# Two-layer hybrid trunk, fp32 as split words: the feed-forward layers in blocks of two weight strips with the activations stationary, in three parts of the inner width, and SBUF opened stage by stage

## The chip, the cores and the metric

The kernel runs on one core of a Trainium2 chip. The metric is the device time of one execution in microseconds (us). The core has five engines that work at the same time and wait for each other by semaphores: TensorE (PE, the matrix array; its weight loads are listed apart as PEld), VectorE (DVE), ScalarE (ACT), GpSimd (POOL) and SyncE (SP, which here only issues DMAs).

## The reference

A decoder trunk of two layers over 256 tokens of width 2048, all float32. Layer 0 mixes by an mLSTM group and a Mamba-2 group from one input projection, layer 1 by causal attention. Each layer ends in a feed-forward layer of inner width 5632, and this is what the change is about:

```python
def rms_norm(x, g):
    y = x * lax.rsqrt(jnp.mean(x * x, axis=-1, keepdims=True) + NORM_EPS)
    return y * g

def swiglu(x, w_gate, w_up, w_down):
    return (jax.nn.silu(x @ w_gate) * (x @ w_up)) @ w_down
...
    x = x + mixer(rms_norm(x, norm_mix[layer]), ...)
    x = x + swiglu(rms_norm(x, norm_ffn[layer]), *ffn_params[layer])
return rms_norm(x, final_norm)
```

## The kernel before

Every matrix product is done with both operands split into a high and a low word, each in a 32-bit format that PE takes in one pass: `wh` is a cast of the weight on ACT (L204), `wl` the remainder on DVE (L205), and activations are split likewise. A product is high times high, high times low and low times high, summed in PSUM. So PE spends three passes on each, and every weight of the 484 MB of matrices is read once, cast once and subtracted once. A chunk is 256 rows by 512 columns of weights (`chunk`, one DMA of 512 KB on SP's queue, four raw buffers, three of `wh` and of `wl`). The normed gain goes into the activations when they are transposed; the factor per token comes after the product.

There are two ways to multiply a chunk. `lin_w` holds the weights stationary: for each 128 weight columns and each 128 rows one matmul of `wh` over 512 columns (high and low words of the 256 tokens side by side, L219) and one of `wl` over 256 columns (L221); the result has channels on partitions, in four banks. `lin_a` holds the activations stationary: for each half of the tokens and each 128 rows three matmuls over the strip's 512 columns (L249 to L251); the result has tokens on partitions, in two banks.

In a feed-forward layer (`ffn`) 11 strips of gate and of up go through `lin_w`, so that the product of the two comes out with channels on partitions, ready to be the stationary operand of the down projection (`project_add` in layer 0, the last loop in layer 1), which is `lin_a` over all 5632 rows for each of four output strips. `project_add` adds the residual (L621), squares the sum on ACT for the next norm (`sq`, L257), transposes the strip on PE (`p_tr`, L169) and, at the end, `row_norm` turns the 256 factors into a row: POOL's power (L110), a diagonal on DVE (`dg`, L188), a matmul with ones (`p_rb`, L189) and a copy.

What is issued in which order is set by the program order together with a scheduler: the weights' casts carry a priority that lets them go ahead of other work of their engine by up to 800 instructions, if their buffers are free, and `later`/`tick` put small jobs (transposes, attention steps) between chunks. SBUF is one pool of 17 blocks of 8 KB per partition (`act`) beside the weight buffers (`stg`), PSUM a ring of six accumulator banks and one of two auxiliary banks. The Mamba gate weights `wg` are set to zero on POOL (L336), loaded by three DMAs of POOL (L338) and split at L341 (`wgh` on ACT, `wgl` on DVE).

## Time and profile before

| | |
|---|---|
| time, median of 3 runs | 2657.42 us (2655.51 to 2658.36) |
| the profiled execution | 2657.61 us |
| its span in the trace | 2655.8 us |
| PE busy | 2634.2 us, 99% of the span |
| DVE, ACT, POOL busy | 61%, 50%, 2% |
| DMA | 187 GB/s on average |
| matmul records on PE | 13765 |
| first matmul of gate/up a, down a, qkv, gate/up b, down b | 787.22, 1287.12, 1529.39, 1916.51, 2407.06 us |

All times of rows are us from the start of the span of that one profiled execution. A matmul's own duration is longer than its share of PE, since matmuls overlap in the array: what one costs is the distance from its start to the next one's start. The chain that ended last shows such shares directly.

### The profile page before, as it was taken

Reading aid. Unit: us, or ns where it says so; the run is one execution under the profiler, and the core shown is the slowest. Engines: PE = TensorE matmul, PEld = TensorE weight load, DVE = VectorE, ACT = ScalarE, POOL = GpSimd, SP = SyncE. Lnnn points to the kernel's source line nnn. Section 1 sums busy time; section 2 is a strip of 40 time slices with the busy share of each in tenths; the row PEclk is TensorE's granted clock in tenths of the full one; section 3 lists DMA queues with packets and bytes.
Section 4 is the critical chain, followed back from the end, with each engine's and each line's share of the span. In section 5 each row is a group of like instructions: output and inputs, shape, how many; then the busy total and the mean of one; then the engine's idle time right before and its main releaser. Section 6 shows DMA issues by size and latency. Waiting matters only on the chain.

```text
span 2655.8 us, 35559 instructions
## 1 busy us (share of the span) xinstructions
PE 2634.2 (99%) x13765; PEld 2246.7 (85%) x13765; DVE 1621.2 (61%) x2128; ACT 1335.1 (50%) x1906; POOL 45.8 (2%) x97
## 2 busy tenths in 40 slices
PE   8999999999999999999999999999999999999998
PEld 7888888888888888888888888888888888888887
DVE  6675687755456666666544466666566666665454
ACT  5465565665444444444444455556444444444443
POOL 1000010000000000000000000000000000000000
PEclk9999999999999999999999999999999999999999
DMA  7565656566555555555555565554556666665554
GB/s 231 168 191 182 184 182 204 167 187 219 189 190 182 185 188 185 188 184 189 190 191 190 190 182 169 177 171 163 185 183 190 190 190 190 190 190 206 193 195 160
DMA packets 254345, 496.86 MB, mean 187 GB/s; under 512 B 15656, under 2 KB 16048, under 8 KB 253792
## 3 DMA queue, kind: packets, MB, share of 16 engines
q1 hardware_dynamic: 250816, 484.57, 57.2%
q0 software_dynamic: 2896, 8.51, 1.1%
q8 instruction: 108, 1.77, 0.3%
q10 hardware_dynamic: 464, 1.52, 0.2%
q14 instruction: 61, 0.50, 0.1%
HBM read 492.39 MB, written 2.14 MB: 186 GB/s over the span
## 4 chain that ended last, share of the span: by engine, by line
PE 97%; DVE 1%; DMA 1%; issue 0%; ACT 0%; POOL 0%; SPq 0%; ACTq 0%; POOLq 0%; DVEq 0%
PE acc_w L219 35%; PE acc_w L221 18%; PE acc_a L249 13%; PE acc_a L251 13%; PE acc_a L250 13%; PE p_tr L169 1%; PE p_y L574 1%; DVE wl L205 1%; PE p_num L451 0%; DMA raw<-in_l_w_in 0%; PE p_qk L689 0%; PE p_o L719 0%; DMA xin<-in_x 0%; ACT wh L204 0%; PE p_pt L711 0%
## 5 line engine op out<-in xcount | busy, mean ns | idle before, releaser
L205 DVE TENSOR_TENSOR wl<-raw,wh 128x1024 fp32r<-128x1024 f32 (+1 forms) x913 | 1116.7, 1223 | 928.0 <-ACT wh L204 923.0
L204 ACT CAST wh<-raw 128x1024 fp32r<-128x1024 f32 (+1 forms) x913 | 958.9, 1050 | 1150.2 <-PE acc_w L219 551.0
L219 PE MATMUL acc_w<-x,wh 128*128 128x512 f32 x3328 | 1170.8, 397 | 0.0
L221 PE MATMUL acc_w<-x,wl 128*128 128x256 f32 x3328 | 929.1, 279 | 0.0
L219 PEld LDWEIGHTS acc_w<-x,wh 128*128 128x128 f32 x3328 | 624.8, 188 | 149.8
L221 PEld LDWEIGHTS acc_w<-x,wl 128*128 128x128 f32 x3328 | 626.9, 188 | 0.5
L219 PE MATMUL acc_w<-xa,wh 128*128 128x512 f32 x768 | 275.8, 403 | 1.1 <-DVE xa L118 1.1
L221 PE MATMUL acc_w<-xa,wl 128*128 128x256 f32 x768 | 215.9, 283 | 0.0
L219 PEld LDWEIGHTS acc_w<-xa,wh 128*128 128x128 f32 x768 | 145.0, 189 | 34.0 <-ACT wh L204 1.5
L249 PE MATMUL acc_a<-wh,xa 128*128 128x512 f32 x384 | 151.5, 395 | 0.0
L250 PE MATMUL acc_a<-wl,xa 128*128 128x512 f32 x384 | 150.8, 393 | 0.0
L251 PE MATMUL acc_a<-wh,xa 128*128 128x512 f32 x384 | 150.7, 393 | 0.0
L221 PEld LDWEIGHTS acc_w<-xa,wl 128*128 128x128 f32 x768 | 145.6, 190 | 1.0
L249 PE MATMUL acc_a<-wh,ha 128*128 128x512 f32 x352 | 137.5, 391 | 0.0
L251 PE MATMUL acc_a<-wh,ha 128*128 128x512 f32 x352 | 137.0, 389 | 0.0
L250 PE MATMUL acc_a<-wl,ha 128*128 128x512 f32 x352 | 137.0, 389 | 0.0
L249 PE MATMUL acc_a<-wh,hb 128*128 128x512 f32 x352 | 136.9, 389 | 0.0
L251 PE MATMUL acc_a<-wh,hb 128*128 128x512 f32 x352 | 136.9, 389 | 0.0
L250 PE MATMUL acc_a<-wl,hb 128*128 128x512 f32 x352 | 136.9, 389 | 0.0
L249 PE MATMUL acc_a<-wh,mx 128*128 128x512 f32 x256 | 100.4, 392 | 0.0
L251 PE MATMUL acc_a<-wh,mx 128*128 128x512 f32 x256 | 99.7, 390 | 0.0
L250 PE MATMUL acc_a<-wl,mx 128*128 128x512 f32 x256 | 99.6, 389 | 0.0
(240 smaller groups left out, 2514.0 us busy)
## 6 DMA issues: line engine op xcount, KB each, us to landing
raw<-in_l_w_in SPq DMA_DIRECT2D x191, 512.0 KB, 3.5
raw<-in_l_ffn_gate SPq DMA_DIRECT2D x176, 512.0 KB, 3.5
raw<-in_l_ffn_up SPq DMA_DIRECT2D x176, 512.0 KB, 3.5
raw<-in_l_ffn_down SPq DMA_DIRECT2D x176, 512.0 KB, 4.4
raw<-in_l_w_qkv SPq DMA_DIRECT2D x96, 512.0 KB, 3.6
raw<-in_l_w_out SPq DMA_DIRECT2D x64, 512.0 KB, 4.6
raw<-in_l_w_o SPq DMA_DIRECT2D x32, 512.0 KB, 3.5
rows<-scr POOLq DMA_DIRECT2D x10, 512.0 KB, 6.0
```

The costliest lines, as they stand in the source:

```text
L169: nc.tensor.transpose(pt[:, j * T + t * P:j * T + (t + 1) * P], src[t][:, c:c + P], ident)
L204: nc.scalar.copy(wh[:, ks, :], raw[:, ks, :])
L205: nc.vector.tensor_sub(wl[:, ks, :], raw[:, ks, :], wh[:, ks, :].bitcast(F32))
L219: nc.tensor.matmul(banks[f], wh[:, kk, fs], kt.both(k), start=k == 0, stop=False, skip_group_check=True)
L221: nc.tensor.matmul(banks[f][:, :T], wl[:, kk, fs], kt.parts(k)[0], start=False, stop=k == nk - 1, skip_group_check=True)
L249: nc.tensor.matmul(banks[t], xh[:, ts], wh[:, kk, :], start=k == 0, stop=False)
L250: nc.tensor.matmul(banks[t], xh[:, ts], wl[:, kk, :], start=False, stop=False)
L251: nc.tensor.matmul(banks[t], xl[:, ts], wh[:, kk, :], start=False, stop=k == nk - 1)
L574: nc.tensor.matmul(py[:, o0:o0 + SHD], e[:, lo:lo + P], y[st][:, hs], start=st == 0, stop=st == t, skip_group_check=True)
```

## The change

Gate and up strips of the same index are done together by `block`: per chunk of 256 rows, one tile of 1 MB is filled by two DMAs of 512 KB (256 rows of the gate strip, 256 of the up strip) and cast in two halves; then for each half of the tokens and each of the two strips, two times three matmuls over 512 columns with the activations stationary. The four products have a fixed bank each (F0 to F3: tokens 0 gate, tokens 0 up, tokens 1 gate, tokens 1 up). The hidden values now have tokens on partitions; so two tanh on ACT (L815) and four operations on DVE (L816, L817) read the banks, and 8 transposes on PE per strip, in two groups of four that are put behind the first chunks of the next block, bring the result back to channels on partitions.

The inner width is done in parts of 4, 4 and 3 strips: hidden values of a part, then the down projection over that part for all four output strips (two blocks of two strips), its result added to the residual after each part. `project_add` remains for `w_out` and `w_o`; the factors per token are used as a column there, so `row_norm` goes after these two. The pools become six long-lived blocks (`res`) and stages m, f, a, g, whose weight buffers and blocks lie over each other's addresses. The final gain is loaded in four pieces on ACT's queue, and the last block takes its last two chunks together. The file also has code for summed weight chunks; with every entry of `PLAN_X` and `PLAN_H` at "P" none of it is run, and it is left out below.

```diff
-    stg = ctx.enter_context(tc.tile_pool(name="stg", bufs=3))
-    act = ctx.enter_context(tc.tile_pool(name="act", bufs=17))
+    res = ctx.enter_context(tc.tile_pool(name="res", bufs=6))
...
-    psa = ctx.enter_context(tc.tile_pool(name="psa", bufs=6, space=PSUM))
-    psx = ctx.enter_context(tc.tile_pool(name="psx", bufs=2, space=PSUM))
+    psm = ctx.enter_context(tc.tile_pool(name="psm", bufs=1, space=PSUM))
...
+    def open_stage(name, act_bufs):
+
+        close_stage()
+        stage["guards"] = [tc.tile_pool(name="stg" + name, bufs=3, reuse_waits="tile"),
+                           tc.tile_pool(name="act" + name, bufs=act_bufs, reuse_waits="tile")]
+        stage["stg"], stage["act"] = [guard.__enter__() for guard in stage["guards"]]
+
     def blk(shape, name, dt=F32):
-        return act.tile(shape, dt, tag="blk", name=name)
+        return stage["act"].tile(shape, dt, tag="blk", name=name)
+
+    def long(shape, name, dt=F32):
+        return res.tile(shape, dt, tag="res", name=name)
 
...
+    def bank(i, name):
+        return psm.tile([P, 512], F32, tag=f"b{i}", name=name)
+
+    def next_bank(kind, name):
+        turn[kind] += 1
+        return bank(ring[kind][(turn[kind] - 1) % len(ring[kind])], name)
+
     def acc_bank(name):
-        return psa.tile([P, 512], F32, tag="acc", name=name)
+        return next_bank("acc", name)
 
     def aux_bank(name):
-        return psx.tile([P, 512], F32, tag="aux", name=name)
+        return next_bank("aux", name)
+
+    open_stage("m", 10)
 
...
+    def weights(src, row, summed):
+
+        pool = stage["stg"]
+        raw = pool.tile([P, 4, STRIP], F32, tag="raw", name="raw", bufs=4)
+        for i, (w, col) in enumerate(src):
+            nc.sync.dma_start(raw[:, 2 * i:2 * i + 2, :],
+                              w[row:row + 2 * P, col:col + STRIP].rearrange("(a p) f -> p a f", p=P))
+
+        def parts(of, cuts):
+            h = pool.tile([P, 4, STRIP], F32R, tag="wh", name="wh")
+            l = pool.tile([P, 4, STRIP], F32R, tag="wl", name="wl")
+            for c in cuts:
+                nc.scalar.copy(h[:, c, :], of[:, c, :])
+            for c in cuts:
+                nc.vector.tensor_sub(l[:, c, :], of[:, c, :], h[:, c, :].bitcast(F32))
+            return h, l
+
+        with tc.high_priority(offset=800):
+            if not summed:
+                return parts(raw, (slice(0, 2), slice(2, 4)))
...
+    def block(src, kt, row, nk, plan, after_sums=None, lead=1):
+        n = nk // 2
+        plan = plan[:n]
...
+        def add(dst, a, b, start, stop):
+            (ah, al), (bh, bl) = a, b
+            nc.tensor.matmul(dst, ah, bh, start=start, stop=False)
+            nc.tensor.matmul(dst, ah, bl, start=False, stop=False)
+            nc.tensor.matmul(dst, al, bh, start=False, stop=stop)
+
...
+                group.append((j, weights(src, row + 2 * j * P, False)))
+                if len(group) < lead and j < n - 1 and n - j <= lead:
+                    continue
+                for i in range(4):
+                    t, s = divmod(i, 2)
+                    first = F[i] is None
+                    if first:
+                        F[i] = bank(i, "acc_f")
+                    for jj, (wh, wl) in group:
+                        for kk in range(2):
+                            xh, xl = kt.parts(2 * jj + kk)
+                            ts = slice(t * P, (t + 1) * P)
+                            add(F[i], (xh[:, ts], xl[:, ts]), (wh[:, 2 * s + kk, :], wl[:, 2 * s + kk, :]),
+                                start=first and jj == group[0][0] and kk == 0, stop=jj == n - 1 and kk == 1)
+                group = []
+            tick()
+        return F, pre
...
+    def col_norm(name, ss4):
+
+        ss = sml.tile([P, NT], F32, tag="ss", name="ss" + name)
+        nc.vector.tensor_reduce(ss, ss4, axis=AX.X, op=OP.add)
+        r = cst.tile([P, NT], F32, name="r" + name)
+        rsqrt_mean(r, ss, D)
+        return r
+
...
+        return nx, col_norm(name, ss)
+
+    def ffn(xt, r, wg_, wu_, wd, name, finish, begin=None):
+
+        rh = cst.tile([P, NT], F32, tag="rh", name="rh" + name)
+        rr = cst.tile([P, NT], F32, tag="rr", name="rr" + name)
+        nc.vector.tensor_scalar(rh, r, 0.5, None, op0=OP.mult)
+        nc.vector.tensor_mul(rr, rh, r)
+
+        def hidden(hT, i, s, plan):
+            F, pre = block(((wg_, s * STRIP), (wu_, s * STRIP)), xt, 0, KD, plan)
+            hs = []
+            for t in range(NT):
+                g, u = F[2 * t], F[2 * t + 1]
...
+                h = t2([P, STRIP], "h")
+                nc.scalar.activation(h, g, AF.Tanh, scale=rh[:, t:t + 1])
+                nc.vector.scalar_tensor_tensor(h, h, 1.0, g, op0=OP.add, op1=OP.mult)
+                nc.vector.scalar_tensor_tensor(h, u, rr[:, t:t + 1], h, op0=OP.mult, op1=OP.mult)
+                hs.append(h)
+            transpose_later(hT, i, hs, None, 1)
+
+        def down(hT, first, n, last):
+            for q in range(2):
+                c0 = 2 * q * STRIP
+                dst = [xr_[t][:, c0 + n_ * STRIP:c0 + (n_ + 1) * STRIP] for t in range(NT) for n_ in range(2)]
+
+                def add_all(what):
+                    for d, x in zip(dst, what):
+                        nc.vector.tensor_add(d, d, x)
+
+                if last and begin is not None:
+                    begin(2 * q)
+                    begin(2 * q + 1)
+                F, _ = block(((wd, c0), (wd, c0 + STRIP)), hT, first * STRIP, 4 * n, PLAN_H, add_all,
+                             lead=2 if last and q and name == "b" else 1)
+                add_all(F)
+                if last:
+                    for s in (2 * q, 2 * q + 1):
+                        finish(s)
+
+        ring["aux"] = (6, 7)
+        first = 0
+        for n in (4, 4, 3):
+            hT = KT(f"h{name}{first}", 4 * n)
...
+            for i in range(n):
+                hidden(hT, i, first + i, PLAN_X if first + i else "P" * len(PLAN_X))
+                ring["aux"] = (4, 5, 6, 7)
+            down(hT, first, n, first + n == DFF // STRIP)
+            first += n
+        ring["aux"] = (6, 7)
+        turn["acc"] = 4
+
+    xt1, r1 = project_add(a["l0_w_out"], mixed, 32, "1", G_FFN0)
+    open_stage("f", 4)
...
+    ffn(xt1, r1, a["l0_ffn_gate"], a["l0_ffn_up"], a["l0_ffn_down"], "a", finish_ffn0)
+    r2, rb2_ = row_norm("2", ss2)
...
+    open_stage("a", 10)
...
+    xt3, r3 = project_add(a["l1_w_o"], oT, KD, "3", G_FFN1)
+    open_stage("g", 4)
+
+
+    gain = {}
+
+    def begin_ffn1(s):
+        gain[s] = stage["stg"].tile([P, STRIP], F32, tag="gf", name="gf", bufs=2)
+        fsrc = a["final_norm"]
+        nc.scalar.dma_start(gain[s], bass.AP(tensor=fsrc.tensor, offset=fsrc.offset + s * STRIP, ap=[[0, P], [1, STRIP]]))
+
     ssf = [cst.tile([P, 4], F32, name=f"ssf{t}") for t in range(NT)]
-    for s in range(4):
-        banks = lin_a(a["l1_ffn_down"], s * STRIP, h1, DFF // P, lead=3 if s == 3 else 1)
+
+    def finish_ffn1(s):
         cs = slice(s * STRIP, (s + 1) * STRIP)
         for t in range(NT):
-            nc.vector.tensor_add(xr_[t][:, cs], xr_[t][:, cs], banks[t])
             sumsq(ssf[t][:, s:s + 1], xr_[t][:, cs])
-            nc.vector.tensor_mul(xr_[t][:, cs], xr_[t][:, cs], gf[:, cs])
+            nc.vector.tensor_mul(xr_[t][:, cs], xr_[t][:, cs], gain[s])
+
+    ffn(xt3, r3, a["l1_ffn_gate"], a["l1_ffn_up"], a["l1_ffn_down"], "b", finish_ffn1, begin_ffn1)
```

On ACT, at the border from `w_out` to the first feed-forward layer (`raw` is the weights as loaded, `xres` the residual, `x13` the transposed last strip). Before:

```order
L204 CAST wh_6924<-raw_6923 128x1024
L204 CAST wh_6969<-raw_6968 128x1024
L204 CAST wh_7001<-raw_7000 128x1024
L204 CAST wh_7032<-raw_7031 128x1024
L257 ACTIVATE sq_6943,ss1_5686<-xres0_5682 128x512
L257 ACTIVATE sq_6945,ss1_5686<-xres1_5683 128x512
L204 CAST wh_7054<-raw_7053 128x1024
```

After:

```order
L266 CAST wh_6928<-raw_6927 128x1024
L418 ACTIVATE sq_6947,ss1_5690<-xres0_5686 128x512
L418 ACTIVATE sq_6949,ss1_5690<-xres1_5687 128x512
L147 ACTIVATE x13_7007<-p_tr_7008,pv_94 128x256
L147 ACTIVATE x13_7007<-p_tr_7050,pv_94 128x256
L147 ACTIVATE x13_7007<-p_tr_7008,pv_94 128x256
L147 ACTIVATE x13_7007<-p_tr_7050,pv_94 128x256
L329 CAST wh_6973<-raw_6970 128x1024 x2
L329 CAST wh_7020<-raw_7017 128x1024 x2
```

The first casts of the feed-forward weights stood ahead of the last squares, and now stand behind them and behind the four splits of the last strip.

On PE, at the same border. Before:

```order
L251 MATMUL acc_a_6633<-wh_6924,mx7_5779 128x512
L219 MATMUL acc_w_6964<-x10_6022,wh_6969 128x512
L221 MATMUL acc_w_6964<-x10_6022,wl_6970 128x256
L219 MATMUL acc_w_6964<-x10_6022,wh_6969 128x512
L221 MATMUL acc_w_6964<-x10_6022,wl_6970 128x256
```

After:

```order
L313 MATMUL acc_a_6637<-wh_6928,mx7_5783 128x512
L202 MATMUL p_tr_7008<-ident_86,xres0_5686 128x128
L202 MATMUL p_tr_7050<-ident_86,xres0_5686 128x128
L202 MATMUL p_tr_7008<-ident_86,xres1_5687 128x128
L202 MATMUL p_tr_7008<-ident_86,xres0_5686 128x128
L202 MATMUL p_tr_7008<-ident_86,xres1_5687 128x128
L202 MATMUL p_tr_7050<-ident_86,xres1_5687 128x128
L202 MATMUL p_tr_7050<-ident_86,xres0_5686 128x128
L202 MATMUL p_tr_7050<-ident_86,xres1_5687 128x128
L357 MATMUL acc_f_6979<-wh_6973,x10_6026 128x512
L357 MATMUL acc_f_6993<-wh_6973,x10_6026 128x512
L358 MATMUL acc_f_6979<-wl_6974,x10_6026 128x512
```

The first feed-forward matmuls stood right behind the last of `w_out`; now the eight transposes of the last strip stand between, and the three words of one product are no longer next to each other at first.

On DVE, some 25 us after the start, in the first input projection (`xa2` is the third strip of the transposed input, `dg` the diagonals, `wgl` the low word of the Mamba gate weights). Before:

```order
L118 SCALAR_TENSOR_TENSOR xa2_222<-p_tr_232,pv_90,xa2_222 128x256
L118 SCALAR_TENSOR_TENSOR xa2_222<-p_tr_223,pv_90,xa2_222 128x256
L188 TENSOR_SCALAR dg_389<-ident_82,r0_384 128x128
L188 TENSOR_SCALAR dg_392<-ident_82,r0_384 128x128
L205 TENSOR_TENSOR wl_283<-raw_281,wh_282 128x1024
L118 SCALAR_TENSOR_TENSOR xa2_222<-p_tr_232,pv_90,xa2_222 128x256
```

After:

```order
L148 SCALAR_TENSOR_TENSOR xa2_226<-p_tr_236,pv_94,xa2_226 128x256
L250 TENSOR_SCALAR dg_393<-ident_86,r0_388 128x128
L250 TENSOR_SCALAR dg_396<-ident_86,r0_388 128x128
L447 TENSOR_SCALAR rh0_401<-r0_388 128x2
L145 TENSOR_TENSOR wgl_1048<-wg_1042,wgh_1047 128x1536
L267 TENSOR_TENSOR wl_287<-raw_285,wh_286 128x1024
L267 TENSOR_TENSOR wl_328<-raw_326,wh_327 128x1024
L148 SCALAR_TENSOR_TENSOR xa2_226<-p_tr_227,pv_94,xa2_226 128x256
```

The subtraction for `wgl`, which came some 60 instructions later, moved in front, and one split of `xa2` moved behind it and two weight subtractions.

## Rows read from the trace of the kernel before

**Rows 1.** The page: busy time and share of the span of each engine, then the chain that ended last by engine, then one group of DMA issues (count, size, median us from issue to landing).

```profile
PE 2634.2 (99%) x13765; PEld 2246.7 (85%) x13765; DVE 1621.2 (61%) x2128; ACT 1335.1 (50%) x1906; POOL 45.8 (2%) x97
...
PE 97%; DVE 1%; DMA 1%; issue 0%; ACT 0%; POOL 0%; SPq 0%; ACTq 0%; POOLq 0%; DVEq 0%
...
raw<-in_l_ffn_gate SPq DMA_DIRECT2D x176, 512.0 KB, 3.5
```

**Rows 2.** PE alone in four stretches, gate/up a, down a, gate/up b, down b: from and to, length, PE busy (matmuls), granted clock, DMA share, GB/s.

```profile
800.00:1280.00 480.00, 480.00 (x2719) 1.00 0.59 186
1300.00:1525.00 225.00, 225.00 (x1005) 1.00 0.57 191
1930.00:2400.00 470.00, 470.00 (x2713) 1.00 0.61 190
2410.00:2640.00 230.00, 230.00 (x1016) 1.00 0.57 192
```

**Rows 3.** Groups of instructions in 800 to 1280 us (gate/up a): line, engine, operation, tiles, shapes, count | busy us, mean ns | idle before.

```profile
L219 PE MATMUL acc_w<-x,wh 128*128 128x512 f32 x1359 | 480.2, 399 | 0.0
L221 PE MATMUL acc_w<-x,wl 128*128 128x256 f32 x1360 | 382.0, 281 | 0.0
L643 DVE TENSOR_TENSOR sg<-sg,rb 128x512 f32<-128x512 f32 x22 | 15.1, 687 | 0.4
L641 ACT ACTIVATE thf<-sg 128x512 f32<-128x512 f32 x22 | 13.9, 630 | 0.6
```

**Rows 4.** The chain that ended last, in down a and at the end of `w_out`: start, length, work.

```profile
787.15 0.24 PE acc_a L251
...
791.41 0.68 PE p_rb L189 x4
...
1349.86 0.44 PE p_tr L169 x4
1353.07 0.44 PE p_tr L169 x4
```

**Rows 5.** The border from `w_out` to gate/up a in order of time: start, length, engine, line, operation [idle before and what ended it].

```profile
784.70 1.05 ACT L204 CAST wh<-raw 128x1024 fp32r<-128x1024 f32 x1 [1.67 <-PE acc_a L251]
...
786.93 1.28 DVE L621 TENSOR_TENSOR xres<-xres,acc_a 128x512 f32<-128x512 f32 x2
...
788.38 0.62 ACT L257 ACTIVATE sq<-xres 128x512 f32<-128x512 f32 x1
788.50 1.22 DVE L205 TENSOR_TENSOR wl<-raw,wh 128x1024 fp32r<-128x1024 f32 x1 [0.30 <-ACT wh L204]
...
791.41 0.68 PE L189 MATMUL p_rb<-dg,ones 128*128 128x128 f32 x4 [0.86 <-DVE dg L188]
...
792.86 0.46 ACT L117 ACTIVATE x<-p_tr,pv 128x256 fp32r<-128x256 f32 x1
...
793.35 0.48 DVE L118 SCALAR_TENSOR_TENSOR x<-p_tr,pv,x 128x256 fp32r<-128x256 f32 x1 [0.75 <-ACT x L117]
```

**Rows 6.** The border from down a to qkv, in the same form.

```profile
1529.10 1.28 DVE L621 TENSOR_TENSOR xres<-xres,acc_a 128x512 f32<-128x512 f32 x2
...
1533.51 0.68 PE L189 MATMUL p_rb<-dg,ones 128*128 128x128 f32 x4 [0.79 <-DVE dg L188]
```

**Rows 7.** The start in order of time, in the same form.

```profile
24.01 0.83 ACT L117 ACTIVATE xa<-p_tr,pv 128x256 fp32r<-128x256 f32 x2
...
25.41 2.09 DVE L188 TENSOR_SCALAR dg<-ident,r 128x128 f32<-128x128 f32 x2
...
25.95 1.40 POOL L336 MEMSET wg<- 128x1536 f32 x1
...
27.42 1.21 DVE L205 TENSOR_TENSOR wl<-raw,wh 128x1024 fp32r<-128x1024 f32 x1
...
27.50 0.40 PE L219 MATMUL acc_w<-xa,wh 128*128 128x512 f32 x1
```

**Rows 8.** The instructions that split the Mamba gate weights, by tile: line, engine, operation and count, duration min/median/max in ns, first and last start, shapes.

```profile
L114 ACT CAST wgh<-wg x1: 1478/1478/1478, 89.9 to 89.9; 128x1536 fp32r<-128x1536 f32 x1
L115 DVE TENSOR_TENSOR wgl<-wg,wgh x1: 1759/1759/1759, 91.4 to 91.4; 128x1536 fp32r<-128x1536 f32 x1
```

**Rows 9.** The chain at the start, in the form of rows 4.

```profile
10.82 2.08 PE acc_w L219 x4
...
13.53 1.28 PE acc_w L219 x3
...
16.98 0.93 PE acc_w L219 x4
```

**Rows 10.** The end of the kernel in order of time, in the form of rows 5.

```profile
2646.22 0.39 PE L251 MATMUL acc_a<-wh,hb 128*128 128x512 f32 x1
2646.65 0.69 DVE L746 TENSOR_TENSOR xres<-xres,acc_a 128x512 f32<-128x512 f32 x1
2647.37 0.63 ACT L257 ACTIVATE sq<-xres 128x512 f32<-128x512 f32 x1 [0.38 <-DVE xres L746]
...
2648.12 0.69 DVE L748 TENSOR_TENSOR xres<-xres,gf 128x512 f32<-128x512 f32 x1 [0.79 <-ACT sq L257]
...
2649.73 1.33 ACT L759 ACTIVATE xres<-xres,rf 128x512 f32<-128x512 f32 x2 [1.64 <-POOL rf L110]
2649.73 0.89 DVE L757 TENSOR_SCALAR xres<-xres,rf 128x512 f32<-128x512 f32 x2 [0.67 <-POOL rf L110]
```

More of the change, by code (lines that the diff above doesn't have):

```diff
@@ L35 @@
 WT = 2
+PLAN_X, PLAN_H = "PPPPPPPP", "PPPPPPPP"
 def _host_constants():
@@ L120, in hybrid_trunk @@
     clock = [0]
+    held = [False]
     pending = []
@@ L136, in tick, with __init__ @@
         clock[0] += 1
-        run_until(lambda p: p[0] > clock[0])
+        run_until(lambda p: held[0] or p[0] > clock[0])
     def need(name):
-        run_until(lambda p: not any(q[2] == name for q in pending))
+        if any(q[2] == name for q in pending):
+            assert not held[0], name
+            run_until(lambda p: not any(q[2] == name for q in pending))
     class KT:
-        def __init__(self, name, n):
-            self.name, self.blocks = name, [None] * (n // 4)
+        def __init__(self, name, n, home=blk):
+            self.name, self.blocks, self.home, self.sums = name, [None] * (n // 4), home, {}
         def block(self, b):
             if self.blocks[b] is None:
-                self.blocks[b] = blk([P, 4, 2, T], f"{self.name}{b}", F32R)
+                self.blocks[b] = self.home([P, 4, 2, T], f"{self.name}{b}", F32R)
             return self.blocks[b]
@@ L194, in chunk @@
     def chunk(w, k, col, step=KC):
[L196 to L198 removed]
+        raw = stage["stg"].tile([P, KC, STRIP], F32, tag="raw", name="raw", bufs=4)
+        wh = stage["stg"].tile([P, KC, STRIP], F32R, tag="wh", name="wh")
+        wl = stage["stg"].tile([P, KC, STRIP], F32R, tag="wl", name="wl")
         for i in range(0, KC, step):
```

154 lines of the change are left out of this document (106 added, 48 removed).

## The prediction

> **What bounds the kernel now.** I read the page first: the busy time and the chain. PE is busy for 99% of the span, and the chain that ended last is PE for 97% [rows 1]. The reader should see in this that no other engine has to be made faster; the time is the sum of what PE issues, plus the few places where PE waits. Then the windows of PE alone, one for each kind of stage: in gate/up and in down PE is busy from edge to edge, at a granted clock of 1.00, while the DMA engines are at about six tenths [rows 2]. So here the cost of a stage is its number of matmuls times their distance. Last I looked where this breaks: the borders between stages [rows 4 to 6], the start [rows 7, 9] and the end [rows 10].
>
> **Gate and up matmuls.** Before, a layer has 11 strips, twice (gate, up), 16 times 128 rows, 4 groups of columns: 1408 pairs of one matmul over 512 and one over 256 columns. From the windows a pair takes 480.00/1359.5 = 353.1 ns in layer a and 470.00/1356.5 = 346.5 ns in layer b [rows 2, 3]. That is 497.1 + 487.9 = 985.0 us. After, the same 768 columns per pair are streamed, but as 1.5 matmuls of 512: 2112 per layer, 4224 in all, of the form that down uses. Down's window b gives 230.00/1016 = 226.4 ns, window a, less six groups of transposes, (225.00 - 2.6)/981 = 226.7 ns [rows 2, 4]; I take 226.6. 4224 x 0.2266 = 957.2 us. Difference: **-27.8 us** (-18.5 if the pairs of layer b were the right measure for both; -30 at 226.0 ns). Down has the same 1056 matmuls per layer as before, and costs the same.
>
> TensorE's own arithmetic in the Trainium skill speaks against this gain ("TensorE: Matmul & The Clock Gate", section "Wait — 56ns, not 53.3ns?"): at full clock the distance is N columns over 2.4 GHz plus about 2.5 ns, so cost goes by columns and the two forms differ only by the 2.5 ns of the matmuls saved. By that page a 512-column matmul would be 215.7 ns and a pair 324.8. The trace disagrees with it on both (226.6, and 353.1 or 346.5). It is a rival below.
>
> **Transposes of the hidden values.** They are new: 11 strips x 2 layers x 8 = 176, in 44 groups of four. A group holds PE for 0.44 us in down a [rows 4]. 44 x 0.44 = **+19.4 us**, all on PE, which has nothing idle to hide it in. Bounds: 17 if the groups run together as the eight at a border do, 22 if each also waits a little for its auxiliary bank.
>
> **Borders w_out to gate/up a, and w_o to gate/up b.** Before, the weights' first casts ran ahead of the border (ACT casts at 784.70), PE went on without a gap, and the only loss was the factor row: PE waits 0.86 us for the diagonal and spends 0.68 us on `p_rb` [rows 5], 1.5 us. That goes. But after, the order of ACT puts the first feed-forward cast behind both squares and four splits, since its buffers lie on those of the stage that ends, and PE has only the eight transposes to do. Working from the end of `w_out` at 787.39 [rows 4]: the adds end at 786.93 + 1.28 = 788.2; the second square and its accumulator read end at about 789.1; four splits of 0.46 on ACT, in turns with 0.48 on DVE over two banks, end at about 791.4; the cast of the first half (1.05, as in 784.70) at 792.5; the subtraction (1.22) at 793.7 [rows 5]. PE's third matmul needs the low word. 793.7 - 787.4 = 6.3, less 0.9 of transposes and 0.45 of two matmuls that can go before: PE waits about 4.95 us, against 1.5: **+3.45 us each**. At the second border two DMA issues on ACT's queue may come in front: +0.7. Bounds for each: -1.5 (the cast is ready after all) to +5. What queues behind the waiting cast on ACT is only later casts, and PE waits for all of those anyway; the second chunk's load waits for the border too, but is needed some 5 us after the first, and 512 KB land in 3.5 [rows 1].
>
> **Border down a to qkv.** `row_norm` stays, and so does its wait [rows 6]. The stage of q, k and v also opens here, so the first cast stands behind the last adds and squares. The same working (two adds of 1.28 in all, a cast, a subtraction) puts the first qkv matmul about 4.3 us behind the end of down, with 0.9 of transposes between; PE idles some 2.95 us against 1.0: **+1.9 us** (bounds 0 to 4).
>
> **The start.** The order moves the subtraction for `wgl` (1.76 us) and two weight subtractions ahead of a split of `xa2`, and the cast for `wgh` (1.48 us) ahead of two weight casts [rows 8, 7]. PE takes that split at 27.50 [rows 7]. ACT, free at about 24.45, casts `wgh` until 25.9, two weights until 28.0, and splits until 28.4; DVE is held by the same (25.9 + 1.76 + 1.2 + 1.2 = 30.1), then splits until 30.5. So PE waits **+3.0 us**, which nothing later gives back. Against it: DVE's `dg`, which took 2.09 us beside POOL's memset [rows 7], is short if the memset comes earlier, as the order of POOL has it; there the memset lies beside DVE's first splits, and the gate weights' DMAs beside the first loads. Bounds 0 to 5.
>
> **The end.** Now the last add is one of four, in two strips, and its multiplication by the gain stands on DVE behind the scaling of the first 128 tokens. Counted from PE's end (2646.45): add until 0.9, square until 1.7, scaling of the first tokens (0.89) until 2.6, multiplication (0.69) until 3.3, then sum and power (from 2648.81 to 2649.73, 0.92) until 4.2, and ACT's two scalings (1.33), if it has done the first tokens', until 5.6 to 6.0. Before it was 2651.06 - 2646.45 = 4.6 [rows 10]: **+1.2 us** (0 to 2.5).
>
> **What I cost at nothing.** The banks between blocks: F0 is finished three banks of six matmuls, 18 x 0.2266 = 4.08 us, before a block ends. It is read by a tanh (0.63) and one DVE operation (0.69) [rows 3], each perhaps behind a weight half (1.05, 1.22 [rows 5]): about 3.1 to 3.9 with the hand-overs. Covered, but by less than 1 us; if the cover goes, each of 34 blocks waits. The residual added three times instead of once, and hidden values by two fewer DVE operations: DVE and ACT have the room [rows 1]. The loads: 1 MB per 24 matmuls (5.44 us) is 193 GB/s, against 186 to 192 now [rows 2].
>
> **Sum.** -27.8 + 19.4 + 3.45 + 4.15 + 1.9 + 3.0 + 1.2 = +5.3 us. Against the profiled execution's 2657.6 us, which is 0.2 above the median of the runs, that gives 2662.9; I predict **2663 us**, its own range 2655 to 2670.
>
> **Rivals.**
> 1. The clock. At the start four 512-column matmuls take 2.08 us, later ones 0.93 [rows 9]: 520 against 233 ns, as 1.2 against 2.4 GHz would make them, though the window's granted clock says 1.00; PE had done little until then. No border of before lets PE wait for as much as 1 us [rows 5, 6], so the trace does not show what a wait of 5 us does. The seven such matmuls of rows 9 took 3.36 us, and at the later distance 1.63. If each of three borders pays 1.7 and the transposes there something too, it is 6 more: 2669 us. The same page of the Trainium skill (section "What's actually happening") says that the array's clock is halved after idling and given back by activity; rows 9 agree.
> 2. The blocks wait. If F0 comes free 0.5 us late, 34 x 0.5 = 17: 2680 us. For it: the margin under 1 us. Against it: DVE and ACT are half idle.
> 3. Cost goes by columns: in gate/up a product streams 768 columns per 128 rows and columns in either form, so at the distances of the pairs (353.1 and 346.5 ns) the first term is nothing: 2662.9 + 27.8 = 2691 us. Against it: two windows of the one form and two of the other. By the page named above, with 2.5 ns for each matmul saved, it would be 3.5 us less than that.
> 4. The other side: ACT and DVE are through sooner than I work out. Where one strip alone ends a stage, the bank of tokens 0 is finished six matmuls, 1.36 us, ahead of that of tokens 1; if its add, square and part of the splits are over by then, and likewise at the start, the first cast ends near 790 and the low word near 791.3. PE then waits 2.5 us at each of the two borders, not 4.95, and the 0.7 and the start's 3.0 go too: 2662.9 - 4.9 - 3.7 = 2654.3 us. The time is not slower than before once 5.5 us of these go. For it: every instruction in that queue is short. Against it: both adds show as one run from 786.93 to 788.2 [rows 5].
>
> **Chances.** Forecast 0.56; rival 1 0.13; rival 2 0.12; rival 3 0.04; rival 4 0.15. The range of 2653 to 2676 leaves out rival 3, most of rival 2 and a small part of rival 4. What a measurement of this kernel can tell from no change is about 0.2%, 5.3 us: faster is under 2652.1, slower over 2662.7. Rival 4 is mostly the same, at its edge faster; the forecast lies on the upper bound, so it gives its chance about evenly to same and slower. Faster 0.09, same 0.38, slower 0.53.
>
> **What will show it.** In gate/up: matmuls at 226 to 227 ns, in a window with no PE idle; were it near 230 or more, or with gaps at every block, the first term or the banks are wrong. Groups of four transposes at 0.44 us. At the borders a PE wait near 5, 3 and 5.5 us, ended by DVE's `wl`. Near 27 us a PE wait of 3 us for a split of `xa2`. Four 512-column matmuls behind a border in 0.9 us, or in 2 if rival 1 is right. The prediction is wrong if gate/up and down of a layer together are not about 4 us shorter than now, or if the borders cost nothing.

## The result and the profile after

The changed kernel takes 2673.36 us (median of 4 runs, 2669.09 to 2675.64), the kernel before 2656.80 (4 runs, 2655.51 to 2658.36): a ratio of 1.006, 95% interval 1.0043 to 1.0078. That is slower, by more than the 0.2% that a measurement can tell. The forecast was 2663 with a range of 2653 to 2676: the direction holds, the value is 10 us short, and the median lies 3 us above the forecast's own range of 2655 to 2670, though within the wide one, which has room for rival 1 too. The profiled execution takes 2669.09 us, with a span of 2667.3.

The page of the changed kernel, in the form of [rows 1]:

```profile
PE 2631.1 (99%) x12525; PEld 2199.4 (82%) x12525; DVE 1500.1 (56%) x1852; ACT 1251.6 (47%) x1726; POOL 47.0 (2%) x97
...
PE 95%; DVE 1%; DMA 1%; ACT 1%; issue 0%; POOL 0%; ACTq 0%; POOLq 0%; DVEq 0%
```

PE is still the bound: busy 3.1 us less than before, in a span 11.5 us longer. So time was lost in waits, and these are in the view of PE's waits by line (us in total, times, longest):

```profile
PE acc_f L357 <- ACT wh L329: 6.2, 2, 3.2
PE acc_w L281 <- DVE xa L148: 3.8, 2, 2.7
...
PE p_tr L202 <- DVE x L148: 2.3, 1, 2.3
PE p_y L735 <- DVE dec L719: 2.0, 1, 2.0
PE p_tr L202 <- DVE xres L792: 1.1, 2, 0.6
PE p_xs L705 <- DVE xsT L666: 0.9, 1, 0.9
...
PE acc_f L358 <- DVE wl L331: 0.8, 2, 0.5
```

The first, the fifth and the last row are the borders behind `w_out` and `w_o`; the second is the start, the third the border to qkv; `p_y` and `p_xs` lie in the first mixer, and the prediction named neither.

The border behind `w_out` in order of time, as in [rows 5]:

```profile
787.01 1.22 DVE L267 TENSOR_TENSOR wl<-raw,wh 128x1024 fp32r<-128x1024 f32 x1 [1.49 <-ACT wh L266]
...
788.26 0.37 SPq L322 DMA_DIRECT2D raw<-in_l_ffn_gate  x1
...
794.83 0.87 PE L202 MATMUL p_tr<-ident,xres 128*128 128x128 f32 x6 [0.56 <-DVE xres L792]
...
797.39 0.47 ACT L147 ACTIVATE x<-p_tr,pv 128x256 fp32r<-128x256 f32 x1 [0.47 <-DVE x L148]
797.77 4.82 ACT L329 CAST wh<-raw 128x1024 fp32r<-128x1024 f32 x5
...
798.85 0.73 PE L357 MATMUL acc_f<-wh,x 128*128 128x512 f32 x2 [3.15 <-ACT wh L329]
...
800.11 0.79 PE L358 MATMUL acc_f<-wl,x 128*128 128x512 f32 x1 [0.53 <-DVE wl L331]
```

Before, PE went straight from `w_out` into the gate matmuls. Now it waits three times: for the add, for the cast that stands behind the splits, and for the low word. The first two rows show how the new buffers follow the old: the new raw buffers lie on the old stage's, and the first feed-forward load goes out when the last `w_out` subtraction has read its chunk (787.01 + 1.22 = 788.23). That load is not what PE waits for here, since the cast starts 9.5 us after its issue; on ACT the last split of the strip (797.39) stands right in front of the cast.

What follows these waits is in the windows of PE (from and to, length, busy and matmuls, granted clock, DMA share, GB/s), the first three at `w_out`, the others at `w_o`:

```profile
796.00:799.80 3.80, 0.73 (x2) 1.00 1.04 399
799.80:803.30 3.50, 3.19 (x8) 0.51 1.05 409
803.30:806.80 3.50, 3.50 (x17) 1.00 1.06 399
1922.00:1926.00 4.00, 0.92 (x7) 1.00 0.78 249
1926.20:1929.70 3.50, 3.19 (x8) 0.51 1.05 397
1929.70:1933.20 3.50, 3.50 (x16) 1.00 1.05 407
```

For some 3.4 us behind each wait the granted clock is the lower of the two levels, 1.2 GHz, and 8 matmuls run where 16 or 17 do in the next window: about 1.7 us lost at each border.

By stage, from the first matmul of one to that of the next (us; each column is one profiled execution, and two experiments that come below stand beside it; the forecast column spreads the terms of the prediction's sum):

| stretch | before | after | difference | forecast | e2_stationary | e10_all_undone |
|---|---|---|---|---|---|---|
| to the first matmul | 10.82 | 10.23 | -0.6 | 0 | 10.53 | 10.53 |
| first mixer, to `w_out` | 598.45 | 604.89 | +6.4 | +3.0 | 597.62 | 599.82 |
| `w_out` to `w_o` (with layer a and attention) | 1209.74 | 1208.36 | -1.4 | -3.4 | 1200.18 | 1200.07 |
| `w_o` to the last matmul (with layer b) | 827.21 | 832.85 | +5.6 | +4.6 | 826.77 | 826.98 |
| behind the last matmul's start | 9.6 | 11.0 | +1.4 | +1.2 | 9.6 | 12.4 |
| span | 2655.8 | 2667.3 | +11.5 | +5.3 | 2644.7 | 2649.8 |

The first mixer, which the change hardly edits, has the largest loss and the largest error of the forecast.

### The profile page after: what moved, and what is told of

The parts are those of the page before. It is cut to its first block, busy times and chain, and to the rows that moved or that the text cites. A ratio compares the mean times of both kernels' runs of the same rounds, so it can differ in the third digit from the quotient of the medians.

```text
span 2667.3 us, 32172 instructions
## 1 busy us (share of the span) xinstructions
PE 2631.1 (99%) x12525; PEld 2199.4 (82%) x12525; DVE 1500.1 (56%) x1852; ACT 1251.6 (47%) x1726; POOL 47.0 (2%) x97
## 4 chain that ended last, share of the span: by engine, by line
PE 95%; DVE 1%; DMA 1%; ACT 1%; issue 0%; POOL 0%; ACTq 0%; POOLq 0%; DVEq 0%
PE acc_f L358 18%; PE acc_f L359 18%; PE acc_f L357 18%; PE acc_w L281 10%; PE acc_a L311 7%; PE acc_a L312 7%; PE acc_a L313 7%; PE acc_w L283 5%; PE p_tr L202 1%; PE p_y L735 1%; DVE wl L267 0%; PE p_num L612 0%; DMA raw<-in_l_w_in 0%; PE p_qk L899 0%; PE p_o L929 0%
## 5 line engine op out<-in xcount | busy, mean ns | idle before, releaser
L331 DVE TENSOR_TENSOR wl<-raw,wh 128x1024 fp32r<-128x1024 f32 x528 | 623.2, 1222 | 693.2 <-ACT wh L329 693.1
L329 ACT CAST wh<-raw 128x1024 fp32r<-128x1024 f32 x528 | 529.2, 1052 | 810.7 <-PE acc_f L359 800.3
L267 DVE TENSOR_TENSOR wl<-raw,wh 128x1024 fp32r<-128x1024 f32 (+1 forms) x385 | 470.0, 1221 | 337.5 <-ACT wh L266 336.2
L266 ACT CAST wh<-raw 128x1024 fp32r<-128x1024 f32 (+1 forms) x385 | 402.8, 1047 | 390.0 <-PE acc_a L313 183.9
L357 PE MATMUL acc_f<-wh,x 128*128 128x512 f32 x1408 | 551.9, 392 | 6.2 <-ACT wh L329 6.2
L358 PE MATMUL acc_f<-wl,x 128*128 128x512 f32 x1408 | 549.3, 390 | 0.8 <-DVE wl L331 0.8
L359 PE MATMUL acc_f<-wh,x 128*128 128x512 f32 x1408 | 549.3, 390 | 0.0
L357 PEld LDWEIGHTS acc_f<-wh,x 128*128 128x128 f32 x1408 | 264.8, 188 | 60.7 <-ACT wh L329 6.7
L359 PEld LDWEIGHTS acc_f<-wh,x 128*128 128x128 f32 x1408 | 265.0, 188 | 55.5
L281 PE MATMUL acc_w<-x,wh 128*128 128x512 f32 x512 | 183.9, 402 | 0.0
L283 PE MATMUL acc_w<-x,wl 128*128 128x256 f32 x512 | 142.9, 280 | 0.0
L357 PE MATMUL acc_f<-wh,ha 128*128 128x512 f32 x352 | 137.7, 391 | 0.0
L359 PE MATMUL acc_f<-wh,ha 128*128 128x512 f32 x352 | 137.0, 389 | 0.0
```

The costliest lines, as they stand in the source:

```text
L266: nc.scalar.copy(wh[:, ks, :], raw[:, ks, :])
L267: nc.vector.tensor_sub(wl[:, ks, :], raw[:, ks, :], wh[:, ks, :].bitcast(F32))
L281: nc.tensor.matmul(banks[f], wh[:, kk, fs], kt.both(k), start=k == 0, stop=False, skip_group_check=True)
L283: nc.tensor.matmul(banks[f][:, :T], wl[:, kk, fs], kt.parts(k)[0], start=False, stop=k == nk - 1, skip_group_check=True)
L329: nc.scalar.copy(h[:, c, :], of[:, c, :])
L331: nc.vector.tensor_sub(l[:, c, :], of[:, c, :], h[:, c, :].bitcast(F32))
```

## The experiments

The theory: the new form of the matmuls gains what was worked out, and four things outside it lose more: the stages laid over each other (borders, and the clock behind them), the early gate split (the wait at 27 us), the smaller block pool in the first mixer (the wait for `dec`), the end. Its rivals: the blocks wait for their banks; the new form gains little or nothing; the one profiled execution is not typical.

**e1_again**: the changed kernel, unaltered.

> The changed kernel once more, unaltered, for its spread and a second trace. Theory: PE's waits at the two borders into the feed-forward layers are long enough to bring the granted clock down to 0.5 for a few us behind each, and in some executions other waits of 2 to 3 us (at 27, 337 and 1532 us) do so too; so this trace again shows the clock low behind both borders, the time lies at 2669 to 2676 us and the ratio near 1.006. Rival: the low clock behind both borders was an accident of one trace; then it is missing at one of them or stands elsewhere.

Measured: 2670.97 us (2669.52 to 2672.75, 6 runs), ratio 1.004 (1.0026 to 1.0055). The waits stand in the same places, though not at the same size: the gap at 385 us is 2.0 us between two matmuls' starts, and 1.3 in the first trace. The low clock behind `w_o` lasts twice as long this time:

```profile
799.90:803.30 3.40, 2.99 (x8) 0.50 1.06 410
1926.30:1929.70 3.40, 2.78 (x6) 0.50 1.05 403
1929.70:1933.10 3.40, 3.40 (x10) 0.50 1.05 403
```

So executions of one kernel differ by how much of the low clock they catch. They differ in a second thing. The same stretch of `lin_w` pairs in qkv, without a gap and at full clock, in the first trace and in this one (windows of PE):

```profile
1540.00:1575.00 35.00, 35.00 (x205) 1.00 0.67 205
```

```profile
1540.00:1575.00 35.00, 35.00 (x201) 1.00 0.65 198
```

From start to start a pair takes 346.7 ns in the first and 353.4 in the second (1550 to 1575 us). The prediction worked the same two paces out of [rows 2], 346.5 ns for layer b and 353.1 for layer a. Here the code is one and the same, so the pace is not a matter of the code alone. What sets it was not tried.

**e2_stationary**: the kernel before, with its pools and stages, and taken from the change only the form of the gate and up matmuls with what it brings along: the transposes of the hidden values, and the factors per token as a column.

```diff
-            banks = lin_w(wg_, s * STRIP, xt, KD)
...
+            gb = lin_a(wg_, s * STRIP, xt, KD)
+            hs = []
+            for t in range(NT):
+                h = t2([P, STRIP], "h")
+                nc.scalar.activation(h, gb[t], AF.Tanh, scale=rh[:, t:t + 1])
+                nc.vector.scalar_tensor_tensor(h, h, 1.0, gb[t], op0=OP.add, op1=OP.mult)
+                hs.append(h)
+            ub = lin_a(wu_, s * STRIP, xt, KD)
+            for t in range(NT):
+                nc.vector.scalar_tensor_tensor(hs[t], ub[t], rr[:, t:t + 1], hs[t], op0=OP.mult, op1=OP.mult)
+            transpose_later(hT, s, hs, None, 1)
```

> The kernel before, with its pools, chunks and order, and with one part of the change alone: gate and up with the activations stationary (two strips one after the other, two banks each), the hidden values transposed on PE, the factors per token as a column after w_out and w_o. Theory: matmuls -28 to -23 us, transposes +19.4, the two factor rows -3, nothing else: 2646 to 2651 us, ratio 0.996 to 0.998, and no low clock after the first 16 us. Rival (cost goes by columns): 2657 + 19 - 3, about 2673 us, ratio 1.006, so that the change's loss would come from here.

Measured: 2646.45 us (2645.46 to 2647.47, 5 runs), ratio 0.9948 (0.9932 to 0.9964): faster than both kernels, and 24.5 us under e1_again on the same chip. Its page and its waits of PE from 700 to 2640 us:

```profile
PE 2624.6 (99%) x12525; PEld 2197.0 (83%) x12525; DVE 1500.6 (57%) x1820; ACT 1279.8 (48%) x1726; POOL 45.8 (2%) x97
```

```profile
PE p_rb L193 <- DVE dg L192: 0.8, 1, 0.8
PE acc_a L253 <- ACT wh L208: 0.5, 1, 0.5
```

From 700 us on it has 1.3 us of waits, against over 10 in the changed kernel. PE has the same 12525 matmuls as the changed kernel, and gate and up take 489.21 us (786.10 to 1275.31) against 499.90 before. The gain of the form is there; the changed kernel loses more elsewhere.

How large the gain is depends on the old form's pace. In layer a, where its pairs took 353 ns, gate and up are 10.7 us shorter; in layer b, at 346.5 ns, only 1.3 (490.55 to 489.22). Over the 1408 pairs of a layer the two paces are 9.4 us apart. The executions of the kernel before stand at about that distance from each other: most near 2657, others near 2666, and one at 2646.18. One layer, none or both at the faster pace would give these times. With one trace of that kernel this is argued, not shown. Against its fastest execution, on another chip, e2 gains nothing.

**e3_gate_late** and **e7_gate_as_before**: the gate weights' memset, and with it their loads and split, held back until a tile of the second strip (e3) or of the third (e7) of the input projection is there.

```diff
     wg = blk([P, KD, 96], "wg")
+    nc.gpsimd.tensor_tensor(wg[:, 0, 0:NT], qT[:, 4, 0:NT], qT[:, 4, 0:NT], op=OP.mult)
     nc.gpsimd.memset(wg, 0.0)
```

e7 has `kT[:, 0, 0:NT]` in place of `qT[:, 4, 0:NT]`.

> The changed kernel with POOL's memset of the Mamba gate weights made to wait for the second strip of q, so that the cast and the subtraction for wgh and wgl no longer stand in front of the splits at 25 us. Theory: PE's wait of 2.7 us at 27 us goes and nothing else changes: 3 us less than the changed kernel beside it (ratio lower by 0.001). Rival: those engines were late for another reason (the first loads), and the wait stays.

> The changed kernel with the Mamba gate weights' memset made to wait for the third strip, which puts the cast of wgh and the subtraction of wgl at the very places of their queues that they had before (in e3_gate_late they came earlier, and PE waited 2.0 us at 75 us instead). Theory: the wait at 27 us goes without a new one: 3 us under the changed kernel. Rival: the wait only moves once more.

Measured: 2672.26 us (2670.73 to 2673.41, 5 runs), ratio 1.0044, and 2670.59 (2668.45 to 2671.69, 5 runs), ratio 1.0047. In both the wait at 27 us is gone and another comes in its place, of PE, at 75.3 and at 98.2 us. The waits of ACT (60 to 90 us in e3, 85 to 110 us in e7) say why:

```profile
ACT wgh L144 <- DMA wg<-in_l_w_in: 5.4, 1, 5.4
```

```profile
ACT wgh L144 <- DMA wg<-in_l_w_in: 5.5, 1, 5.5
```

The cast for `wgh` sits at its place in ACT's queue until its DMAs land, and the weight casts queue behind it. Neither run could price the wait at 27 us, since each made a new one, and the low clock stood at other places too (e3 at 338.7 and 1536.8 us, e7 at 340.5). They show that the split must be held back behind its loads, not the loads alone.

**e4_one_pool**: one weight pool for all stages, so that casts run ahead across a border; to fit, a tile is 128 rows of two strips, and the transposes, the gain's buffers and the last block's lead are fitted to that.

```diff
-        close_stage()
+        if stage:
+            return
...
-        raw = pool.tile([P, 4, STRIP], F32, tag="raw", name="raw", bufs=4)
+        raw = pool.tile([P, KC, STRIP], F32, tag="raw", name="raw", bufs=4)
...
+            nc.sync.dma_start(raw[:, i, :], w[row:row + P, col:col + STRIP])
...
+            nc.scalar.copy(h, raw)
+            nc.vector.tensor_sub(l, raw, h.bitcast(F32))
```

> The changed kernel with one set of weight buffers for the whole program, of 4 KB per partition as before, never closed and opened again: a feed-forward chunk is 128 rows of two strips instead of 256 (two DMAs of 256 KB, one cast), the transposes of the hidden values two and three of these chunks later, the last three chunks taken together, the final gain in temporary tiles. Theory: the border waits come from the stages' buffers lying over each other; here the first casts stand ahead of the border again, so PE's waits there fall under 1 us, the clock stays up, and the time is 2 x 5 + 2 = 12 us or more under the changed kernel: 2657 to 2661 us. Rival: the waits come from the squares and splits of the last strip, whichever buffers are used; then the time stays at 2667 or above.

Measured: 2673.05 us (2670.83 to 2676.26, 6 runs), ratio 1.0048 (1.0031 to 1.0066): no gain. Yet the waits at the two borders are gone, and the clock stays at 1.00 there. In their place the waits have two new groups (PE, and its weight loads):

```profile
PE acc_f L337 <- DVE h L760: 6.2, 22, 0.3
```

```profile
PEld acc_f L337 <- DVE h L760: 15.5, 22, 0.7
```

All 22 blocks of gate and up wait for the bank that the block before has just filled. With 128 rows per chunk the first bank is finished only three banks of three matmuls, 9 x 0.2266 = 2.04 us, ahead of a block's end, not 18. A block's first matmuls stand 672 ns apart there, 0.45 more than a free one; the same 768 matmuls and 6 groups of transposes take 179.37 us (1063.60 to 1242.97) against 177.04 in the changed kernel. The theory had the borders right and the time wrong: the prediction's rival 2 had moved in.

**e5_two_chunks**: e4 with the last two chunks of every block taken together, so that 18 matmuls follow the first bank again.

```diff
-            if len(group) < lead and k < nk - 1 and nk - k <= lead:
+            if len(group) < max(lead, 2) and k < nk - 1 and nk - k <= max(lead, 2):
```

> The kernel of e4_one_pool with the last two chunks of every block taken together, so that 18 matmuls follow the last one into bank F0 instead of 9. In e4's trace the border waits and the low clock behind them are gone, but the time is not, and at block ends a matmul starts 0.67 us after the one before, 0.45 us more than usual. Theory: the next block waits for F0; 34 x 0.45 = 15 us go, and the time is 2655 to 2660 us. Rival: the half-size chunks cost in themselves (smaller DMAs, twice the hand-overs), and the time stays at 2670.

Measured: 2658.13 us (2655.12 to 2661.14, 11 runs), ratio 1.000 (0.9992 to 1.0009). The stretch is back at 177.03 us (1060.10 to 1237.13), and both borders run without a gap (windows of PE):

```profile
790.00:794.00 4.00, 4.00 (x20) 1.00 0.68 235
794.00:798.00 4.00, 4.00 (x21) 1.00 0.48 147
1909.00:1913.00 4.00, 4.00 (x19) 1.00 0.72 241
```

That is 15 us less than e4 by one line, which acts on the blocks' ends alone, and 13 less than e1_again (both on another chip, where the kernel before took 2658.47 us against 2657.43 here). The 34 x 0.45 of the expectation meets the number partly by luck: only the 22 blocks of gate and up waited, and the stretch of four of them was 2.34 us longer in e4, of which their waits explain 1.8.

**e6_eleven_blocks**: the first stage's pool with 11 blocks, not 10.

```diff
-    open_stage("m", 10)
+    open_stage("m", 11)
```

> The changed kernel with 11 blocks instead of 10 in the first stage, which is what SBUF has room for. Before, the decay rows of the first x strip were loaded at 300 us; in the changed kernel POOL waits for a block until 329 us, the load meets the weights' loads, and PE waits 2.0 us at 337 us and longer than before at 386. Theory: with the eleventh block the load stands where it was, both waits go back to what they were before, and 3 to 4 us of the changed kernel's time with them: ratio lower by 0.001 to 0.0015. Rival: the weights' loads are late there for another reason, and both waits stay.

Measured: 2669.39 us (2667.05 to 2670.48, 5 runs), ratio 1.0041 (1.0027 to 1.0055). The wait for `dec` is not in its list of waits. POOL's issues of the decay rows in the changed kernel, and then in e6, say why:

```profile
329.40 1.54 POOL L566 DMA_DIRECT2D rows<-scr  x2 [32.38 <-PE p_xs L705]
```

```profile
306.64 1.53 POOL L566 DMA_DIRECT2D rows<-scr  x2 [6.26 <-PE p_cb L689]
```

With 10 blocks, `rows` has to wait for a block that `p_xs` still reads, and comes 23 us later than with 11. The gain in the median, 1.6 us under e1_again on another chip, is about the size of that wait and too small to prove it by itself; the rows do. The second half of the theory fails: the wait of `p_xs` near 386 us is 0.9 us with 11 blocks as with 10. And in this trace the clock is low from 29.6 to 36.4 us, behind the wait at the start.

**e8_all_undone**: e5 with 11 blocks and the memset held as in e7.

> All of it together: one pool of weight buffers, the last two chunks of a block together, eleven blocks, the gate weights at their old place; what is left of the change is the blocks of two strips, the three parts and the transposes. Theory: from the 2657 us of before, matmuls and transposes -6, two factor rows -3, the end +1.5 to +3: 2650 to 2653 us, no low clock between 16 us and the end, near to e2_stationary and some 4 us above it. Rival: the three parts and the blocks of two strips cost something more that no wait shows; then it stays above 2656.

Measured: 2654.23 us (2653.19 to 2655.28, 11 runs), ratio 0.9991 (0.9982 to 1.0000): 1 to 4 us above what was expected, and under the rival's 2656. Its trace has e7's wait of 2 us, at 97.9, with a granted clock of 0.50 from 99.7 to 103.2.

**e9_gate_split_late**: the loads of the gate weights left as early as in the changed kernel, only their split held back. The added instruction writes zeros into two columns of padding.

```diff
+    nc.gpsimd.tensor_tensor(wg[:, 0, 0:NT], r0_, r0_, op=OP.mult)
     nc.gpsimd.memset(wg, 0.0)
...
+    nc.gpsimd.tensor_scalar(wg[:, 0, 8:10], kT[:, 0, 0:NT], 0.0, None, op0=OP.mult)
```

> The changed kernel with the Mamba gate weights loaded as before (memset behind POOL's first power) and only their split made to wait for the third strip, by a product with 0.0 that POOL writes into two of the columns that are zero. In e7_gate_as_before the wait at 27 us was gone, but the cast of wgh waited 5.5 us for the load that the edit had made late, and PE 2.0 us at 98 us. Theory: now neither wait is there; about 3 us under the changed kernel (2668 us or less, ratio near 1.0035). Rival: the split of the gate weights costs PE a wait wherever it stands in this kernel; then one of 2 us or more is found again before 110 us.

Measured: 2668.62 us (2666.59 to 2672.83, 12 runs), 0.6 us above the 2668 expected and 2.4 under e1_again. On this chip most executions of the kernel before lay near 2666 at the same granted clock (17 runs, 2656.27 to 2667.57, median 2665.74; ratio 1.0022), so times here are set against the changed kernel and not as ratios. Neither wait is left before 127 us. The four executions with a mean granted clock of 0.994 take 2671.46 to 2672.83 us, the four with 0.997 take 2666.59 to 2668.77. The trace is of the former kind (windows of PE, behind the wait for `dec` and behind the border to qkv):

```profile
336.10:339.50 3.40, 3.40 (x16) 0.50 0.64 180
339.50:342.90 3.40, 3.40 (x15) 0.50 0.92 340
...
1534.20:1537.60 3.40, 3.08 (x11) 0.50 0.10 13
```

So gaps of 2.3 and 2.6 us between two matmuls' starts can bring the low clock too; in the profiled execution of the changed kernel they did not.

**e10_all_undone**: e5, 11 blocks, and the gate split of e9.

> e8_all_undone with the gate weights as in e9_gate_split_late. Theory: the wait of 2.0 us at 98 us and the low clock behind it in e8's trace go: 2650 to 2652 us, and between 16 us and the end no low clock. What is left above e2_stationary (2646) is the end of the kernel, 12.4 against 9.6 us behind the last matmul. Rival: it stays at 2654, and the difference to e2 lies in the blocks.

Measured: 2651.35 us (2650.26 to 2651.88, 6 runs), as expected, and the granted clock is 1.00 from 16 to 2641 us. All its waits of PE behind the first loads:

```profile
PE acc_w L282 <- DVE xa L149: 1.1, 1, 1.1
PE p_cols L499 <- ACT colsrc L490: 0.9, 1, 0.9
PE p_rb L252 <- DVE dg L251: 0.6, 1, 0.6
PE acc_a L312 <- ACT wh L267: 0.5, 1, 0.5
PE p_xs L651 <- DVE xsT L612: 0.4, 1, 0.4
PE acc_a L312 <- ACT zh L697: 0.2, 1, 0.2
```

The changed way of multiplying in blocks and parts, with the losses outside it taken away, is some 20 us under the changed kernel (2670.97 in e1_again, on another chip). In the table it matches e2 to 0.2 us in both stretches from `w_out` to the last matmul. What it has over e2 is 2.2 us in the first mixer and 2.8 behind the last matmul; the causes of these two were not tried. Part of the first is the pace of the old form's pairs (352.7 ns against 347.5 from 30 to 80 us). The faster version of the two is e2.

## Why the prediction was right and where it was wrong

**The matmuls (-27.8): right for the execution that was read.** In the changed kernel 768 matmuls and 24 transposes fill a stretch without a gap, as the matmuls of before do in [rows 2]:

```profile
1066.20:1243.20 177.00, 177.00 (x793) 1.00 0.58 190
```

A matmul's median distance there is 227 ns, its mean away from the transposes 226.9 to 227.0, against the 226.6 taken. The price of the old form is not as firm: the prediction read 353.1 and 346.5 ns for the same instructions in two layers and added them up without asking why they differ. Its bound of -18.5 is the case in which both layers run at the faster pace. Rival 3, cost by columns, is refuted by e2, which has the new form and little else new: 12.0 us less in gate and up of both layers, of which some 3 are the factor rows, with the transposes already paid. An estimate from the arithmetic by columns of the Trainium skill ("TensorE: Matmul & The Clock Gate", section "Wait — 56ns, not 53.3ns?"), 1408 matmuls fewer at 2.5 ns, would have left a gain of 3.5 us in both layers together, before any transpose is paid.

**The transposes (+19.4): right.** From the starts in that stretch a group takes 0.45 to 0.46 us from its neighbours, against 0.44. With the 0.3 ns by which each of 4224 matmuls is further apart than taken, about 2 us are missing from the two terms together.

**The borders of `w_out` and `w_o` (+3.45 and +4.15): mechanism, place and size right, the consequence missed.** The waits listed add up to 4.24 us at the first border (0.56 + 3.15 + 0.53), most of it ended by the cast and only 0.53 by the low word that the prediction named as its sign, and PE's gaps with the hand-overs to 4.7, against 4.95 worked out. The 0.7 for the gain's issues is not there. That the wait also costs the clock was priced as rival 1 and left out of the sum: 1.7 us at each, as the windows show, and rival 1 had 1.7 for each border. It should have been in the sum, not beside it. e5, with no waits there, has 1.00. The halving after idling that the prediction cites beside rival 1 (the Trainium skill, "TensorE: Matmul & The Clock Gate", section "What's actually happening") agrees with these windows.

**Border to qkv (+1.9): the size about right, the mechanism not.** PE's gap there is 2.61 us against 1.07, so +1.5. But PE does not wait for the new stage's cast or subtraction: the wait of 2.3 us is that of a transpose, ended by the split `x` on DVE (third row of the waits above), and the splits stand between the squares on ACT.

**The start (+3.0): right.** PE's gap at 26.6 us is 2.97, behind the rows forecast (start, length, as in [rows 7]):

```profile
25.13 1.76 DVE L145 TENSOR_TENSOR wgl<-wg,wgh 128x1536 fp32r<-128x1536 f32 x1
26.81 2.35 DVE L267 TENSOR_TENSOR wl<-raw,wh 128x1024 fp32r<-128x1024 f32 x2
29.08 0.87 DVE L148 SCALAR_TENSOR_TENSOR xa<-p_tr,pv,xa 128x256 fp32r<-128x256 f32 x2
29.61 0.51 PE L281 MATMUL acc_w<-xa,wh 128*128 128x512 f32 x1 [2.69 <-DVE xa L148]
```

e9 takes it away with that split alone.

**The end (+1.2): right**, +1.4.

**The step that was missing: the pools.** "What I cost at nothing" has the banks, the residual, the hidden values and the loads, but not the 17 blocks that become 10 in the first stage, beside six long-lived ones. No row was read for when its buffers come free. That is the gap at 336.8, 2.4 us from start to start and 2.2 more than the usual distance, of the 3.4 us that the first mixer is off; e6 shows its cause. Two other gaps, 0.4 longer than before at 385.7 and 0.3 at 131.4, are not the pool's as far as the runs show: with 11 blocks both are still there in e6 (1.24 and 1.21 us). Their cause stays open.

**The sum.** In the profiled execution 6.2 us are missing from the forecast: 3.4 from the clock at two borders, 2.2 from the pool, 0.7 from the two other gaps, about 2 from matmuls and transposes, 0.2 at the end; against them stand -0.7 of issues, -0.6 at the first matmul, -0.4 at qkv and about -0.5 at the two borders. That leaves 6.3, and the old form's pace in the first mixer and in qkv moves some tenths each way.

The largest piece is the clock, which the prediction had priced and given 0.13. That its wide range holds the result is partly luck: the pool, which no term and no rival has, fell into the room left for the clock.

The sign that gate/up and down of a layer would be about 4 us shorter came true only on average: from the first gate matmul to the last of down, layer a is 9.4 us shorter and layer b 0.7 longer, each with 1.7 us of low clock in it.

The median of the runs is 4.3 us above the profiled execution, which was the fastest of the four. The three others have granted clocks of 0.994 to 0.996 against 0.997. That this spread is the clock's is shown for traces (e1_again, e9), not for each execution.

**Rival 2** did not come about in the changed kernel, whose waits of PE have no row for a block that waits for `h`, and e4 shows how near it was: with 2.04 us of cover a block waits 0.45, so the reader needs about 2.5 us by this estimate, not the 3.1 to 3.9 worked out, and the cover of 4.08 was ample. **Rival 4** fell: ACT and DVE were not early at any of the three places.

## What to carry to other kernels

Pools that are reopened over each other's addresses make the first load, cast and wait of the new stage follow the last use of the old one: keep the weight buffers across stages if the bound engine has no other work there, or price the gap and then the clock behind it. When a chunk is made smaller, count the matmuls that still run behind the first finished bank, since that cover is paid for in every block. When a pool shrinks, look for loads in unrelated stages that get their buffer from it, and before taking over a large rearrangement try its core alone in the old frame: here that was 24.5 us faster than the whole on one chip (2646.45 against 2670.97). And when the same instructions run at two paces in one trace, ask which of them the price is.

## What the runs showed that was not expected

- The low clock behind a wait is not the same from execution to execution. The gaps of 3.4 us between matmuls' starts at the borders brought it in all six traces that have them, for 3.4 or 6.8 us. Shorter ones did and did not: near 336 us gaps of 1.9 (e3), 2.1 (e4), 2.3 (e9) and 2.5 (e7) brought it, but 2.4 in the changed kernel's profiled execution, 2.3 in e5 and 1.9 in e1 did not; at 27 us a gap of 3.0 brought it in e6 and not in four others; at the border to qkv 2.6 brought it in e3 and e9 and not in four others; 2.0 near 98 us brought it in e8 and not in e7.
- The pairs of the old form run at 346.7 or 353.4 ns, at full clock and without a gap, and the same stretch of the same kernel takes one or the other in different executions. The 512-column matmuls of the new form do not show this: gate and up take 489.21 and 489.22 us in the two layers of e2.
- The kernel before has executions near 2666 us and one at 2646.18 beside those near 2657, at the same mean clock of 0.999. The two paces would explain the distances; no trace of such an execution shows it.
